# One of four weight sums per quad formed by a plain load and an accumulating transfer instead of a VectorE add

## The chip, the cores and the metric

The kernel runs on one core of one Trainium2 chip. The metric is the device time of one execution in microseconds (us), the median over several runs. The engines are called by the profile's names: PE (TensorE matmul), PEld (TensorE weight load), DVE (VectorE), ACT (ScalarE), POOL (GpSimd), SP (SyncE; SPq is its queue of instructions that issue transfers).

## The reference, cut to what matters

Two layers of a hybrid encoder on 592 tokens (528 of a new stream, 64 of a running one), model width 1024. Each layer is a feed-forward block, a token mixer and a second feed-forward block, all float32. Only the feed-forward blocks meet the change:

```
def _swiglu(x, w_gate, w_up, w_down):
    return (jax.nn.silu(x @ w_gate) * (x @ w_up)) @ w_down
...
h = h + 0.5 * _swiglu(_rmsnorm(h, ln_ffa_w[l]), ffa_w_gate[l], ffa_w_up[l], ffa_w_down[l])
```

`w_gate` and `w_up` are 1024 x 2816, `w_down` is 2816 x 1024.

## The kernel before

**Seven products in place of eight.** Most of a feed-forward block is cast as 2 x 2 blocks of products and computed with seven block products instead of eight (a Strassen-Winograd scheme). One such group is a *quad* (class `Quad`, line 439). For the up side a quad makes one 128-wide column of gate and of up for both halves of the tokens; for the down side it makes two columns of the output. The four blocks of weights of a quad are g1, g2 (`wg`) and u1, u2 (`wu`), each 128 partitions by `nk` slices of 128 floats; `nk` is 4 on the up side, 3 or 2 on the down side. The seven products need seven weights: the raw g1, g2, u2 and four sums, s1 = u1+u2, s2 = s1+g1, s4 = s2+g2, s3 = g1+u1. They are used in the order of `QUAD`: g1, s1, s2, s4, s3, g2, u2, so s3 is the fifth. There are 20 up quads in each of four feed-forward blocks, and 16, 16, 16 and 12 down quads: 140 in all, 80 with nk = 4, 48 with nk = 3, 12 with nk = 2.

**From HBM to PE.** `fetch_quad` (line 568) loads g1, u1, u2, g2 from SP's queue into `braw` (six buffers; the trace calls them wr, the loads are at line 574). `combine` (line 584) forms the four sums on DVE (line 588) into `bzq` (four buffers; the trace calls the sums ws). `convert` (line 593) splits each of the seven weights into a rounded part on ACT (wh, line 603, six buffers) and a remainder on DVE (wl, line 607, six buffers). `product_quad` (line 666) multiplies: for each slice three matmuls of 296 columns (288 in the last block), hi x hi, hi x lo, lo x hi (lines 680 to 682), so 21 x nk matmuls for a quad. A product is accumulated in PSUM onto an earlier one; the next product into the same accumulator is held by a gate until an engine has read the intermediate value (DVE at lines 909 and 1018, ACT at 888 to 898). Those readers stand in DVE's queue among the sums and the remainders.

**Order.** Every engine works its instructions in the order in which they were written. That order comes from a planner (class `Plan`): each piece of work is a generator that yields an engine, an assumed duration, the events that it waits for and the buffers that it needs, and the planner always takes the task that could start first, by its assumed times (a DMA of a slice 190 ns, landing 2000 ns later, a DVE pass 67 ns + n/0.96). On the chip an instruction waits by semaphores for what it needs, and all behind it on its engine wait with it. `bzq` is also used in the token mixers, which hold no quads. POOL's queue holds little in the feed-forward blocks: a power function at each norm, and scaling in the last one.

Of the kernel before, what the change touches and what calls it, by code (L numbers as in the profile page):

```python
# [13 lines left out]
ALU = mybir.AluOpType  # L14
PSUM = bass.MemoryType.PSUM

P = 128
# [18 lines left out]


BLK = ((0, 128), (128, 128), (256, 128), (384, 128), (512, 80))
NT = 52
UK = 4  # L40
LEVELS = (64, 32, 16, 8, 4, 2, 1)

# [73 lines left out]
def ns_dve(n):  # L116
    return 67 + n / 0.96
# [80 lines left out]
def body(ctx: ExitStack, tc: tile.TileContext, a: dict, o: dict):  # L198
    nc = tc.nc
    V, S, G, PE, SP = nc.vector, nc.scalar, nc.gpsimd, nc.tensor, nc.sync  # L200
# [5 lines left out]
    plan = Plan({PE: (200.0, 60.0), V: (220.0, 0.0), S: (265.0, 0.0), G: (100.0, 0.0)}, {G: V})  # L206
    bT = Buf(sb, "T", NT, [P, T], F32, 6)
    bhw = Buf(sb, "hw", 6, [P, HT], F32)
    bzq = Buf(sb, "zq", 4, [P, T], F32)
    braw = Buf(sb, "raw", 6, [P, UK, P], F32)  # L210
# [192 lines left out]
    def near(order):  # L403
        return 1e-3 * order
# [50 lines left out]
    class Mix:  # L455
# [18 lines left out]
        def combine(self, j, x1, x2, y, evs, done):  # L474


            n = self.n
            lo, hi = slice(0, n), slice(n, 2 * n)
            t = yield V, 3 * ns_dve(n), (evs[0], evs[1], evs[3])
            V.tensor_tensor(y[:, lo], x2[:, hi], x1[:, hi], op=ALU.subtract)  # L480
            V.tensor_tensor(x1[:, hi], x1[:, lo], x1[:, hi], op=ALU.subtract)
            V.scalar_tensor_tensor(y[:, hi], x1[:, hi], -1.0, x2[:, hi], op0=ALU.mult, op1=ALU.subtract)
            ends = []
            for p, src, w in ((0, x1, t), (1, y, t), (2, x2, evs[2])):
                ends.append(Ev())
                plan.add(near(self.order + 2 * p), self.split(p, j, src[:, :2 * n], t, w, ends[-1]))
            t = yield V, ns_dve(n), (ends[0], evs[2])
            V.scalar_tensor_tensor(x1[:, lo], y[:, hi], -1.0, x2[:, lo], op0=ALU.mult, op1=ALU.subtract)
            yield "none", 0, (t, ends[1])
            done[2](max(t, ends[1].t))  # L490
            e4 = Ev()
            plan.add(near(self.order + 6), self.split(3, j, x1[:, lo], t, t, e4))
            yield "none", 0, (t, ends[2])
            done[1](max(t, ends[2].t))
            yield "none", 0, (e4,)
            done[0](e4.t)
# [14 lines left out]
    def fetch():  # L511
# [9 lines left out]
        for i, job in enumerate(jobs):  # L521
            if isinstance(job, Quad):
                yield from fetch_quad(i, job, chain)
                continue
            src = job.src.rearrange("(k p) c -> p k c", p=P)
            for k0, k1, u in job.units:
                if job.whole:
                    if i == 0:
                        yield from whole(i, job, src, k0, k1, u, chain)
                    else:  # L530
                        plan.add(near(job.order), whole(i, job, src, k0, k1, u, chain))
                    if i == 0:
                        for b, g in ((0, 1), (1, 1), (2, 1)) if k0 == 0 else ():
                            yield from fetch_x(b, g)
                    continue
                t = yield "DMA", 190 * (k1 - k0), (), (braw,)
                raw = braw.tile(f"wr{i}", [P, k1 - k0, src.shape[2]])
                SP.dma_start(raw, src[:, k0:k1])
                t += 2000.0
                if job.few:  # L540
                    plan.add(near(job.order), convert_few(i, job, u, raw, t, chain))
                else:
                    plan.add(near(job.order), convert(u, raw, chain, braw.put, t))
            if i == 1:
                for b, g in ((3, 0), (4, 0), (3, 1), (4, 1)):
                    yield from fetch_x(b, g)
                t = yield "DMA", 380, ()
                SP.dma_start(cf[:, P:], a["c_f"][:, P:3 * P])
                cf_ev.set(t + 2000)
                load_params()  # L550
# [17 lines left out]
    def fetch_quad(i, job, chain):  # L568
        nk = job.mix.nk
        got = {}  # L570
        for name, src in (("g1", job.wg[0]), ("u1", job.wu[0]), ("u2", job.wu[1]), ("g2", job.wg[1])):
            t = yield "DMA", 190 * nk, (), (braw,)
            raw = braw.tile(f"wr{i}", [P, nk, P])
            SP.dma_start(raw, src)
            got[name] = [raw, Ev(), Ev({"g1": 3}.get(name, 2), braw.put)]
            got[name][1].set(t + 2000.0)
        for name, n in (("s1", 2), ("s2", 2), ("s4", 1), ("s3", 1)):
            got[name] = [None, Ev(), Ev(n, bzq.put)]
        plan.add(near(job.order), combine(i, nk, got))
        for k, ((name, _, _), u) in enumerate(zip(QUAD, job.units)):  # L580
            raw, ev, use = got[name]
            plan.add(near(job.order + k), convert(u, got[name], chain, use.set, ev))

    def combine(i, nk, got):
        for name, p, q in (("s1", "u1", "u2"), ("s2", "s1", "g1"), ("s4", "s2", "g2"), ("s3", "g1", "u1")):
            t = yield V, ns_dve(nk * P), (got[p][1], got[q][1]), (bzq,)
            dst = got[name][0] = bzq.tile(f"ws{i}", [P, nk, P])
            V.tensor_tensor(dst, got[p][0], got[q][0], op=ALU.add)  # L588
            got[name][1].set(t)
            got[p][2].set(t)  # L590
            got[q][2].set(t)

    def convert(u, raw, chain, done, *waits):

        prev, chain[0] = chain[0], Ev()
        split = chain[0]
        n = u.n * P
        t = yield S, ns_act(n), (*waits, prev) if prev else waits, (bhi,)
        if isinstance(raw, list):
            raw = raw[0]  # L600
        u.hi = bhi.tile("wh")
        hi = u.hi[:, :u.n]
        S.activation(hi, raw, AF.Copy)  # L603
        split.set(0.0)
        t = yield V, ns_dve(n), (t,), (blo,)
        u.lo = blo.tile("wl")
        V.tensor_tensor(u.lo[:, :u.n], raw, hi.bitcast(F32), op=ALU.subtract)  # L607
        done(t)
        u.ready.set(t)
# [447 lines left out]
    for e in range(2):  # L1057
        t = const.tile([P, 5 * P], F32, name=f"att{e}")
# [944 lines left out]
```

## Time and profile before

| | |
|---|---|
| median of 3 runs | 2339.91 us (2338.31 to 2341.12) |
| profiled execution, its own time | 2347.44 us |
| span in the profile | 2345.7 us |
| mean granted TensorE clock | 0.992 |
| PE busy | 2271.2 us (97%) |
| DVE busy | 2026.8 us (86%) |
| ACT busy | 1213.5 us (52%) |
| POOL busy | 122.5 us (5%) |
| DMA engines' share | 27.9% (185.50 MB on SP's queue) |

The profiled execution lies 7.5 us over the median, and its span 1.7 us below its own time. Busy times are shares of the span; matmuls overlap each other in the records, so a gap of less than about 0.16 us between two matmuls doesn't show as idle time of PE.

### The profile page before, as it was taken

To read this page: it belongs to the slowest core of one execution; us is meant where nothing else is said; L and a number is where in the kernel's file an instruction comes from. 1 tells how busy PE (TensorE), PEld (TensorE's weight loads), DVE (VectorE), ACT (ScalarE), POOL (GpSimd) and SP (SyncE) were. 2 spreads that over 40 slices of the span, in tenths; PEclk is the share of its full clock that TensorE was granted. 3 is DMA by queue.
4 is the path that set the end of the run, shared out by engine and by line. 5 is a ranking of instruction groups with operands and counts; after the bars stand their busy time and mean duration, and the time that the engine had idled before them with its cause. 6 is when DMAs were issued, how large, how long until landed. Compare 5 with 4: busy or idle time off the path is not lost.

```text
span 2345.7 us, 43539 instructions
## 1 busy us (share of the span) xinstructions
PE 2271.2 (97%) x16199; PEld 2186.0 (93%) x16199; DVE 2026.8 (86%) x4224; ACT 1213.5 (52%) x2488; POOL 122.5 (5%) x167
## 2 busy tenths in 40 slices
PE   8989999999899999999999999999998999999998
PEld 6989999999899899999979999999997998999998
DVE  6989989768976899998989999896789678998995
ACT  4555646446443355564545556464563534554653
POOL 0000000021300000000000000000212000000002
PEclk9999999999999999999999999999999999999999
DMA  4232232332112123323223323323311221333232
GB/s 119 83 96 86 86 95 77 95 80 60 28 46 82 54 82 100 91 82 100 75 70 88 100 84 91 90 80 92 81 44 33 64 86 50 89 101 90 86 96 76
DMA packets 370243, 188.28 MB, mean 80 GB/s; under 512 B 16544, under 2 KB 367568, under 8 KB 370032
## 3 DMA queue, kind: packets, MB, share of 16 engines
q1 hardware_dynamic: 370032, 185.50, 27.9%
q8 instruction: 128, 2.10, 0.4%
q14 instruction: 83, 0.68, 0.1%
HBM read 180.94 MB, written 4.51 MB: 79 GB/s over the span
## 4 chain that ended last, share of the span: by engine, by line
PE 55%; DVE 32%; DMA 7%; issue 4%; ACT 1%; SPq 0%; POOL 0%; DVEq 0%; ACTq 0%
DVE wl L607 8%; PE pq L680 6%; PE pq L682 6%; PE pq L681 6%; DVE ws L588 5%; PE pd L680 3%; DVE h L1018 3%; PE pd L681 3%; PE pd L682 3%; DMA wr<-in_ffa_w_up 2%; DMA wr<-in_ffb_w_up 2%; DVE ql_g L505 2%; PE pa L1385 2%; PE px L654 1%; PE px L656 1%
## 5 line engine op out<-in xcount | busy, mean ns | idle before, releaser
L603 ACT ACTIVATE wh<-ws 128x512 fp32r<-128x512 f32 (+2 forms) x560 | 321.4, 575 | 274.2 <-PE pd L681 119.4
L603 ACT ACTIVATE wh<-wr 128x512 fp32r<-128x512 f32 (+2 forms) x572 | 333.0, 587 | 222.9 <-PE pd L681 89.4
L607 DVE TENSOR_TENSOR wl<-wr,wh 128x512 fp32r<-128x512 f32 (+2 forms) x572 | 358.1, 639 | 6.8 <-ACT wh L603 4.9
L607 DVE TENSOR_TENSOR wl<-ws,wh 128x512 fp32r<-128x512 f32 (+2 forms) x560 | 338.5, 615 | 20.2 <-ACT wh L603 19.1
L680 PE MATMUL pd<-qh_g,wh 128*128 128x296 f32 (+1 forms) x1008 | 306.8, 304 | 11.7 <-DVE h L1018 9.5
L681 PE MATMUL pd<-ql_g,wh 128*128 128x296 f32 (+1 forms) x1008 | 301.9, 300 | 4.1 <-DVE ql_g L505 4.1
L682 PE MATMUL pd<-qh_g,wl 128*128 128x296 f32 (+1 forms) x1008 | 301.2, 299 | 0.0
L680 PE MATMUL pq<-qh_a,wh 128*128 128x296 f32 x960 | 287.8, 300 | 0.7 <-ACT gg L898 0.7
L682 PE MATMUL pq<-qh_a,wl 128*128 128x296 f32 x960 | 286.5, 298 | 0.9 <-DVE wl L607 0.9
L681 PE MATMUL pq<-ql_a,wh 128*128 128x296 f32 x960 | 286.9, 299 | 0.2 <-DVE ql_a L505 0.2
L682 PE MATMUL pq<-qh_b,wl 128*128 128x296 f32 (+1 forms) x960 | 285.0, 297 | 1.0 <-DVE wl L607 0.9
L680 PE MATMUL pq<-qh_b,wh 128*128 128x296 f32 (+1 forms) x960 | 285.6, 298 | 0.0
L681 PE MATMUL pq<-ql_b,wh 128*128 128x296 f32 (+1 forms) x960 | 285.6, 297 | 0.0
L588 DVE TENSOR_TENSOR ws<-wr,wr 128x512 f32<-128x512 f32 (+2 forms) x280 | 172.5, 616 | 48.7 <-DMA wr<-in_ffa_w_up 21.9
L680 PEld LDWEIGHTS pd<-qh_g,wh 128*128 128x128 f32 x1008 | 191.0, 189 | 21.7 <-issue 14.5
L1018 DVE SCALAR_TENSOR_TENSOR h<-pd,h 128x296 f32<-128x296 f32 (+1 forms) x420 | 191.4, 457 | 11.6 <-PE pd L682 10.8
L681 PEld LDWEIGHTS pd<-ql_g,wh 128*128 128x128 f32 x1008 | 191.4, 190 | 4.7 <-DVE ql_g L505 4.7
L682 PEld LDWEIGHTS pd<-qh_g,wl 128*128 128x128 f32 x1008 | 191.1, 190 | 0.0
L681 PEld LDWEIGHTS pq<-ql_a,wh 128*128 128x128 f32 x960 | 180.9, 188 | 1.4 <-DVE ql_a L505 1.2
L682 PEld LDWEIGHTS pq<-qh_a,wl 128*128 128x128 f32 x960 | 180.7, 188 | 1.5 <-DVE wl L607 1.5
L682 PEld LDWEIGHTS pq<-qh_b,wl 128*128 128x128 f32 x960 | 180.5, 188 | 1.7 <-DVE wl L607 1.7
L681 PEld LDWEIGHTS pq<-ql_b,wh 128*128 128x128 f32 x960 | 180.7, 188 | 1.1 <-DVE ql_b L505 1.0
(468 smaller groups left out, 5606.7 us busy)
## 6 DMA issues: line engine op xcount, KB each, us to landing
wr<-in_w_in SPq DMA_DIRECT2D x112, 256.0 KB, 3.1
wr<-in_ffa_w_gate SPq DMA_DIRECT2D x88, 256.0 KB, 3.0
wr<-in_ffa_w_up SPq DMA_DIRECT2D x88, 256.0 KB, 3.2
wr<-in_ffb_w_gate SPq DMA_DIRECT2D x88, 256.0 KB, 3.0
wr<-in_ffb_w_up SPq DMA_DIRECT2D x88, 256.0 KB, 3.2
wr<-in_ffa_w_down SPq DMA_DIRECT2D x96, 192.0 KB, 2.8
wr<-in_ffb_w_down SPq DMA_DIRECT2D x96, 192.0 KB, 2.7
wr<-in_w_out SPq DMA_DIRECT2D x32, 256.0 KB, 3.0
```

The lines of the kernel that those rows point to most:

```text
L505: V.tensor_tensor(ql, src, qh.bitcast(F32), op=ALU.subtract)
L588: V.tensor_tensor(dst, got[p][0], got[q][0], op=ALU.add)
L603: S.activation(hi, raw, AF.Copy)
L607: V.tensor_tensor(u.lo[:, :u.n], raw, hi.bitcast(F32), op=ALU.subtract)
L654: PE.matmul(out[:, :n], u.hi[:, i], xh, start=(j == 0), stop=False)
L656: PE.matmul(out[:, :n], u.lo[:, i], xh, start=False, stop=(j == nk - 1))
L680: PE.matmul(out, u.hi[:, j], xh, start=(new and j == 0), stop=False, skip_group_check=True)
L681: PE.matmul(out, u.hi[:, j], xl, start=False, stop=False, skip_group_check=True)
L682: PE.matmul(out, u.lo[:, j], xh, start=False, stop=(j == nk - 1), skip_group_check=True)
L1018: V.scalar_tensor_tensor(dst, sums[b], sign, dst, op0=ALU.mult, op1=ALU.add)
L1385: PE.matmul(pt[:n, c0 // 2:(c0 + n) // 2], ks[:, c0:c0 + n], qs[:, c0 // 2:(c0 + n) // 2], start=True, stop=True)
```

## The change

The sum s3 leaves `combine`. A new task `load_sum` for each quad takes a `bzq` buffer, loads u1 (`wu[0]`) into it by a plain transfer from SP's queue, and then issues from POOL's queue a second transfer of g1 (`wg[0]`) from HBM with `accum_op=ALU.add` onto the same buffer. The tasks are chained: the first transfer of one isn't planned before that of the task ahead of it (`before`, `after`). In the planner the first counts 190 ns a slice on the DMA, the second is ready 2500 ns later, counts 1000 ns on POOL, and s3 counts as there 4500 ns after that. g1 now has two readers instead of three and u1 one instead of two. For the descriptors of POOL's transfers 2048 bytes a partition are reserved instead of 256, and the pool `T` of general buffers (592 floats a partition each) has 51 instead of 52. The planner is run anew, so the order of all engines can come out otherwise.

```diff
-NT = 52
+NT = 51
...
-            got[name] = [raw, Ev(), Ev({"g1": 3}.get(name, 2), braw.put)]
+            got[name] = [raw, Ev(), Ev({"u1": 1}.get(name, 2), braw.put)]
             got[name][1].set(t + 2000.0)
         for name, n in (("s1", 2), ("s2", 2), ("s4", 1), ("s3", 1)):
             got[name] = [None, Ev(), Ev(n, bzq.put)]
+        prev, sums[0] = sums[0], Ev()
+        plan.add(near(job.order), load_sum(i, nk, job.wu[0], job.wg[0], got["s3"], prev, sums[0]))
         plan.add(near(job.order), combine(i, nk, got))
...
+    sums, begun = [Ev(0)], []
+
+    def load_sum(i, nk, first, second, to, before, after):
+
+        t = yield "DMA", 190 * nk, (before,), (bzq,)
+        dst = to[0] = bzq.tile(f"wa{i}", [P, nk, P])
+        SP.dma_start(dst, first)
+        after.set(0.0)
+        t = yield G, 1000, (t + 2500.0,)
+        G.dma_start(dst, second, accum_op=ALU.add)
+        to[1].set(t + 4500.0)
+
     def combine(i, nk, got):
-        for name, p, q in (("s1", "u1", "u2"), ("s2", "s1", "g1"), ("s4", "s2", "g2"), ("s3", "g1", "u1")):
+        for name, p, q in (("s1", "u1", "u2"), ("s2", "s1", "g1"), ("s4", "s2", "g2")):
...
-    nc = _bacc.Bacc("TRN2", target_bir_lowering=False, num_devices=1, dynamic_dma_scratch_size=256)
+    nc = _bacc.Bacc("TRN2", target_bir_lowering=False, num_devices=1, dynamic_dma_scratch_size=2048)
```

## Rows read from the trace of the kernel before

**Rows 1.** Windows view, four quad stretches: length; busy us (count) PE, PEld, DVE, ACT, POOL; clock; DMA
```profile
53.78:435.54 381.76, 365.46 (x2606) 357.56 (x2605) 351.74 (x739) 216.06 (x432) 1.35 (x4) 0.99 0.30 87
817.26:1186.52 369.26, 363.07 (x2607) 356.16 (x2606) 347.49 (x714) 202.56 (x406) 0.00 (x0) 1.00 0.31 91
1224.33:1594.98 370.65, 363.62 (x2606) 357.01 (x2605) 351.00 (x722) 210.94 (x425) 0.00 (x0) 1.00 0.30 88
1971.45:2305.22 333.77, 328.19 (x2438) 323.66 (x2437) 311.73 (x622) 185.06 (x364) 0.00 (x0) 1.00 0.32 92
sum 1455.44, PE 1420.35 PEld 1394.39 DVE 1361.97 ACT 814.62 POOL 1.35; mean PE 355.09 PEld 348.60 DVE 340.49 ACT 203.66 POOL 0.34
```

**Rows 2.** Timeline of PE inside one stretch: start us, duration us
```profile
1290.04 0.30 PE L680 MATMUL pd<-qh_g,wh 128*128 128x296 f32 x1
...
1291.26 0.30 PE L680 MATMUL pd<-qh_g,wh 128*128 128x296 f32 x1
```

**Rows 3.** Waits of PE: us in total, times, longest us
```profile
PE pd L680 <- DVE h L1018: 13.6, 15, 6.4
PE pq L680 <- DVE u L909: 9.6, 17, 2.5
...
PE pd L681 <- DVE ql_g L505: 4.1, 3, 1.7
```

**Rows 4.** Windows view just after the long stall, and the matmul that ended it
```profile
149.00:152.00 3.00, 2.73 (x11) 2.76 (x12) 2.30 (x6) 0.34 (x1) 0.00 (x0) 0.50 0.59 171
...
149.27 0.58 PE L680 MATMUL pd<-qh_g,wh 128*128 128x296 f32 x1 [6.40 <-DVE h L1018]
```

**Rows 5.** Waits of DVE
```profile
DVE ws L588 <- DMA wr<-in_ffa_w_up: 21.9, 16, 6.6
...
DVE ws L588 <- DMA wr<-in_ffb_w_up: 16.7, 19, 3.5
```

**Rows 6.** Waits of SPq and of ACT
```profile
SPq L574 <- DVE wl L607: 734.9, 232, 16.8
...
ACT wh L603 <- PE pd L681: 208.8, 305, 5.1
```

**Rows 7.** Timeline of DVE: a sum and its follower, four and three slices
```profile
268.26 0.69 DVE L588 TENSOR_TENSOR ws<-wr,wr 128x512 f32<-128x512 f32 x1
268.86 0.69 DVE L607 TENSOR_TENSOR wl<-wr,wh 128x512 fp32r<-128x512 f32 x1
...
1151.13 0.55 DVE L588 TENSOR_TENSOR ws<-wr,wr 128x384 f32<-128x384 f32 x1
1151.60 0.77 DVE L505 TENSOR_TENSOR ql_g<-gg,qh_g 128x592 fp32r<-128x592 f32 x1
```

**Rows 8.** DMA issues: SPq instruction count, KB each, median us from issue to landing
```profile
wr<-in_ffa_w_up SPq DMA_DIRECT2D x88, 256.0 KB, 3.2
...
x<-in_x_prompt SPq DMA_DIRECT2D x6, 256.0 KB, 7.0
```

**Rows 9.** DMA queues: packets, MB, share of 16 engines
```profile
q1 hardware_dynamic: 370032, 185.50, 27.9%
```

**Rows 10.** Timeline of DVE and POOL in the first mixer
```profile
568.89 2.44 POOL L1515 TENSOR_TENSOR st_o<-st_o,mhalf 128x4 f32<-128x4 f32 x2 [28.71 <-DVE st_o L1512]
...
569.34 0.77 DVE L1265 TENSOR_TENSOR l<-l,l 128x592 f32<-128x592 f32 x1
...
572.72 0.83 DVE L1276 SCALAR_TENSOR_TENSOR cmk<-cmk,lnc,cum 128x592 f32<-128x592 f32 x1
...
599.47 1.03 POOL L1681 TENSOR_TENSOR ls<-cf,lah 128x512 fp32r<-128x512 f32 x1
...
600.05 6.08 DVE L1276 SCALAR_TENSOR_TENSOR cmk<-cmk,lnc,cum 128x592 f32<-128x592 f32 x1
...
604.47 1.03 POOL L1681 TENSOR_TENSOR ls<-cf,lal 128x512 fp32r<-128x512 f32 x1
```

## The prediction

> **What bounds the kernel now.** The change touches only quads, so I looked first for the time that quads take. The windows view cut at the first and last quad matmul of each feed-forward block gives four stretches of 381.8, 369.3, 370.7 and 333.8 us, 1455.4 us of the 2345.7 us span; the reader is to see that PE is busy 1420.4 us and DVE 1362.0 us of them, both near full, and POOL 1.35 us [rows 1]. The rest, mixers and norms, has no quad.
>
> The second view is PE's timeline in a spot without gaps. Nine matmuls take 1291.26 - 1290.04 = 1.22 us, so 0.1356 us each at 296 columns [rows 2]. A block has 20 x 4 x 21 up and (3+2+3+3) x 4 x 21 down matmuls, 2604, or 353.1 us at that pace; the last block has 2436, which at 288/296 of the pace is an estimated 321.4 us. Sum 1380.7 us: PE alone would need that. The stretches lose 1455.4 - 1380.7 = 74.7 us over it, and no relief of DVE can give back more than this.
>
> The third view is what PE waited for. In the stretches it is nearly always DVE: the accumulation into h (13.6 us), the reader u (9.6 us), the remainders ql_g (4.1 us) [rows 3]. One of these waits is 6.4 us, and the 3 us behind it run at 0.50 of the granted clock, TensorE's 1.2 GHz level, after that idleness [rows 4]. It stands in the first block, where DVE waited 6.6 us for u1 and u2 behind a burst of small parameter loads [rows 5]. That is about 6.4 + 1.5 = 8 us which a saved add doesn't touch. So some 67 us are open to the change; 27.3 - 6.4 = 20.9 us of them show as waits for those three, the rest lies in gaps that overlapping records hide.
>
> The fourth view is what DVE waited for: 38.6 us of the sums' own wait for u1 and u2 [rows 5]. So DVE has little slack, and a good part of it is transfers that come late, in front of a sum, with the readers of PSUM queued behind. SP's loads in turn wait for `braw` buffers that a remainder on DVE frees (734.9 us, all harmless as long as loads are ahead) [rows 6].
>
> **The change, part by part.**
>
> *Removed: 140 adds on DVE.* The add on four slices starts at 268.26 and its follower at 268.86: 0.60 us. On three slices it is 1151.13 to 1151.60: 0.47 us [rows 7]. Two slices are one step less, an estimated 0.34 us. 80 x 0.60 + 48 x 0.47 + 12 x 0.34 = 48.0 + 22.6 + 4.1 = 74.7 us of DVE, 5.5% of its 1362.0 us. This is DVE time, not kernel time.
>
> *Moved: the release of raw buffers.* u1's buffer comes free after s1 instead of after s3, g1's after s2 and its conversion. The next quad's first load can start earlier; but u2, which s1 needs, is only third in the queue and still waits for a third buffer. I count this as nothing in the sum, and as what pays for busier DMA engines.
>
> *Added on SP: 140 plain loads of u1.* SPq idles for most of a stretch in waits for buffers [rows 6], so issuing is free unless a load stands in front of a raw load while waiting for its `bzq` buffer. Behind it then stand g1, u1, u2, g2 of the next quad, and DVE's s1 waits for those.
>
> *Added on the DMA engines.* 370032 packets took 27.9% of 16 engines in 2345.7 us, 28.3 ns each [rows 9]. Each new operand has 488 slices x 128 partitions = 62464 packets, 110 us of all 16 engines. For the accumulating one I bound the price from once to twice that (it must also fetch what it adds to), 110 to 221 us; together 220 to 331 us in 1455 us of stretches. The share there rises from 0.31 to between 0.46 and 0.54 [rows 1]: no bound by itself, but a raw load that takes 3.2 us from issue to landing [rows 8] can find half of one more in its way. I charge 5 us, with a range of nothing to 25 us: 0.18 us on each of 140 quads at most, of which DVE's slack takes most.
>
> *Added on POOL: 140 instructions that issue the second transfer.* The trace of before has none. Lower bound nothing; nearest rows are POOL's own instructions, 1.03 us for a 512-wide product and 2.44/2 = 1.22 us for a power [rows 10]. At 1.2 us they are 168 us on an engine that is idle in the stretches. The power at each norm stands in the same queue; it waits at most for one such transfer's u1 (3.2 us), five times, when no quad is close: nothing taken, 16 us as far end.
>
> *The chain of one s3.* Plain load 3.2 us [rows 8], POOL 0 to 1.2 us, accumulating transfer between 3.2 us (a plain one) and 7.0 us (the same 256 KB while the start of the kernel loads x) [rows 8]: 6.4 to 11.4 us. I take 8.5 us, nearer the quiet row, because the DMA share stays near a half. A quad lasts 84 x 0.1356 = 11.4 us on PE with nk = 4, 8.5 us with 3, 5.7 us with 2. So the sum has to be started about a quad ahead, in one of four `bzq` buffers, and then the other three sums have fewer to run ahead in. What covers a late s3 is that conversions run ahead of PE: ACT waited 208.8 us for PE to free a weight buffer [rows 6], which it only does when it is six weights ahead, and s3 is one in seven.
>
> *One buffer fewer in `T`.* No row shows a wait for one. Nothing taken; up to 5 us as an estimate of one stalled hand-over per mixer and norm.
>
> *How DVE's relief reaches PE.* If every us of DVE counted, it would give 67 us (PE is then the bound); if only what DVE would have done in its idle time moves, nothing. DVE's queue delays PE in the visible 20.9 us and in hidden gaps; 5.5% less work for an engine that is 94% busy should remove more than a third of the queueing. I take 25 us of the 67, the visible waits and a little more. Sum: 25 - 5 = 20 us off 2347.4 us, so 2327 us for an execution like the profiled one; against the median, which is 7.5 us lower, 2339.9 - 20 = 2320 us.
>
> *POOL against DVE.* In the mixer a DVE instruction with SBUF operands that takes 0.83 us lasted 6.08 us while POOL ran six products of 1.03 us back to back: DVE stood still for as long as POOL streamed. Beside POOL's powers on 4 columns, 2.44 us long, a DVE product took its usual 0.77 us [rows 10]. So it is streaming that blocks, not a busy POOL, and a transfer's issue streams no tensor; I take no blocking. [...]
>
> **The rivals.**
>
> 1. *Larger gain.* The late readers were the whole loss: 35 to 60 us, 2280 to 2305 us. For it: DVE is 94% busy in the stretches [rows 1]. Against: 38.6 us of DVE's idleness waits for transfers, which get no quicker [rows 5].
> 2. *No change.* The freed DVE time becomes waiting for u1 and u2, because the extra traffic delays them by about as much as the add cost (0.5 us a quad). 2335 to 2345 us.
> 3. *Slower: s3 comes late.* If the chain lasts 10 us and runs one buffer at a time, down quads stretch: 48 x (10 - 8.5) + 12 x (10 - 5.7) = 72 + 52 = 124 us, less the gain of 20: about 2440 us. At 9 us it is 24 + 40 - 20 = 44 us, 2384 us. It decides against the change from about 8.7 us, if the planner can't keep two buffers on it. Against it: the conversions' lead.
> 4. *Slower: POOL holds DVE while it writes descriptors, or the reverse.* By the mixer's rows an instruction on POOL costs DVE (6.08 - 0.83)/6 = 0.88 us [rows 10]; 140 x 0.88 = 123 us, less the saved 74.7, is 48 us more for DVE. At one for one that is 2388 us. The break-even is 74.7/140 = 0.53 us a transfer.
>
> **How the numbers follow.** My forecast, 10 to 32 us faster: 0.45, range 2308 to 2330 us. Rival 1: 0.15. Rival 2: 0.14. Rival 3: 0.16. Rival 4: 0.10. 0.2% (4.7 us) is about what a measurement of this kernel can tell from no change: faster 0.45 + 0.15 = 0.60, same 0.14, slower 0.26. The range for eight in ten runs from 2288 us, which leaves out the far end of rival 1 (0.05), to 2385 us, which leaves out half of each slower rival (0.13).
>
> **What would show it.** DVE's sums at the line of `combine` fall from 560 to 420 and its busy time by about 75 us. The four stretches shrink to some 1435 us together, and PE's waits for h and u with them. POOL has 140 more instructions, and DVE's products beside them keep their 0.6 to 0.7 us; longer ones mean rival 4. ACT's conversion of s3 should show no wait for a transfer; if it does, and PE waits for that weight, it is rival 3. DVE's wait for u1 and u2 above 60 us would be rival 2. The prediction fails if the accumulating transfer lands more than about 5 us after its issue while only one buffer serves it.

## The result, and the profile after

The changed kernel takes 2321.7 us (median of 4 runs, 2317.44 to 2327.99), the kernel before 2340.51 us beside it (2338.31 to 2342.73): a ratio of 0.9922 with an interval of 0.9894 to 0.995. Five more rounds gave 2319.07 us and 0.9912 (0.99 to 0.9924), 20.6 us off. The profiled execution took 2317.44 us, its span is 2315.7 us. The profile of before came from an execution 7.5 us above its median, so the two spans lie 30.0 us apart, more than the gain; sizes below go by ratios, and the spans serve to find places.

The windows view of after, cut as in [rows 1]:

```profile
52.99:429.20 376.21, 363.13 (x2606) 357.94 (x2605) 340.05 (x705) 219.00 (x434) 46.29 (x39) 0.99 0.56 129
805.35:1169.66 364.31, 359.15 (x2606) 354.75 (x2605) 336.50 (x681) 203.54 (x407) 46.08 (x36) 1.00 0.58 136
1204.20:1571.55 367.35, 360.36 (x2607) 354.69 (x2605) 339.01 (x691) 211.76 (x428) 44.80 (x35) 1.00 0.57 131
1946.13:2274.47 328.34, 325.85 (x2439) 323.20 (x2437) 299.07 (x591) 185.43 (x364) 39.96 (x31) 1.00 0.59 139
sum 1436.21, PE 1408.49 PEld 1390.57 DVE 1314.63 ACT 819.72 POOL 177.14; mean PE 352.12 PEld 347.64 DVE 328.66 ACT 204.93 POOL 44.28
```

The stretches shrink from 1455.4 to 1436.2 us. Over the 1380.7 us that PE alone would need, they lose 55.5 us where they lost 74.7. DVE is busy 47.3 us less in them, and the share of the DMA engines has gone from 0.31 to 0.57.

Outside the stretches the two spans differ by another 30.0 - 19.2 = 10.8 us, though no sum of a quad lies there. A part of it is the clock at the seam behind the first block (before, then after; PE alone):

```profile
440.00:445.00 5.00, 2.99 (x20) 0.90 0.51 127
445.00:450.00 5.00, 5.00 (x22) 0.50 0.28 83
```

```profile
434.00:439.00 5.00, 3.73 (x29) 1.00 0.77 210
439.00:444.00 5.00, 5.00 (x39) 1.00 0.19 51
```

Before, PE is idle for 2.0 of 5 us there, and the 5 us behind it show a granted clock of 0.50; after, it is idle for 1.3 us, and the 5 us behind it show 1.00. In another execution of the changed kernel PE is idle there for the same 1.3 us, and the 5 us behind it show 0.71; DVE goes 7.52 us there from st_m (L714) to its first q (L1087), 6.02 us in the profile of after. So this part differs from one execution to the next.

What the prediction calls the 1.2 GHz level behind the long stall is, as far as the trace of before shows it, the 0.50 of [rows 4] and a pace: ten matmuls of 296 columns take 2.46 us there, 1.20 columns a ns, where the nine of [rows 2] take 1.22 us, 2.18 columns a ns.

```profile
149.90 0.45 PE L682 MATMUL pd<-qh_g,wl 128*128 128x296 f32 x1
...
152.36 0.45 PE L680 MATMUL pd<-qh_g,wh 128*128 128x296 f32 x1
```

What PE waited for (answers to [rows 3]: the same accumulations, the line numbers 14 higher), then what DVE waited for [rows 5], and what ACT waited for where a transfer of s3 was late:

```profile
PE pq L694 <- DVE u L923: 9.0, 8, 3.1
PE pd L694 <- DVE h L1032: 8.3, 11, 1.9
...
PE pd L695 <- DVE ql_g L505: 3.1, 3, 1.1
PE pq L694 <- ACT gg L902: 2.9, 3, 1.7
```

```profile
DVE wl L621 <- ACT wh L617: 57.6, 76, 1.4
...
DVE ws L602 <- DMA wr<-in_ffa_w_up: 11.0, 15, 2.2
...
DVE ws L602 <- DMA wr<-in_ffb_w_up: 6.1, 9, 2.1
```

```profile
ACT wh L617 <- DMA wa<-in_ffb_w_gate: 11.0, 4, 4.1
...
ACT wh L617 <- DMA wa<-in_ffa_w_gate: 9.4, 4, 2.9
```

PE's three waits fall from 27.3 to 20.4 us; the single stall of 6.4 us [rows 4] is gone as one piece. DVE waits 17.1 us for u1 and u2 where it waited 38.6, and 57.6 us for ACT's rounded weights, where the row of before is

```profile
DVE wl L607 <- ACT wh L603: 24.0, 36, 2.0
```

DVE now reaches a remainder more often before ACT has made its operand, which is what an engine with spare time looks like. ACT waited 23.0 us, nine times, for an s3 that wasn't there yet: 20.4 us in the eight waits of the two rows shown, and one of 2.6 us on the down side. PE shows no wait for a converted weight. But ACT also reads intermediate values for PE, and those reads stand in the same queue. Behind the two longest waits for s3 they came late, and PE stood still for them, 2.6 of its 2.9 us in that row:

```profile
973.20 0.63 ACT L617 ACTIVATE wh<-wa 128x512 fp32r<-128x512 f32 x1 [4.00 <-DMA wa<-in_ffb_w_gate]
...
974.25 0.40 ACT L902 ACTIVATE gg<-pq 128x296 f32<-128x296 f32 x1
...
974.70 0.40 PE L694 MATMUL pq<-qh_b,wh 128*128 128x296 f32 x1 [0.89 <-ACT gg L902]
...
1971.86 0.63 ACT L617 ACTIVATE wh<-wa 128x512 fp32r<-128x512 f32 x1 [4.05 <-DMA wa<-in_ffb_w_gate]
...
1974.40 0.39 ACT L902 ACTIVATE gg<-pq 128x288 f32<-128x288 f32 x1
...
1974.84 0.41 PE L694 MATMUL pq<-qh_b,wh 128*128 128x288 f32 x1 [1.74 <-ACT gg L902]
```

The queues and the issues of after (SP's queue is q1, POOL's q0; for issues the count, KB each and median us from issue to landing):

```profile
q1 hardware_dynamic: 434736, 217.49, 33.5%
q0 software_dynamic: 64704, 31.99, 11.3%
...
wr<-in_ffa_w_up SPq DMA_DIRECT2D x88, 256.0 KB, 3.6
...
wa<-in_ffa_w_up SPq DMA_DIRECT2D x40, 256.0 KB, 3.6
wa<-in_ffa_w_gate POOLq DMA_DIRECT2D x40, 256.0 KB, 4.9
```

An accumulating packet takes 0.113 x 16 x 2315.7 / 64704 = 64.7 ns of an engine, a plain one 0.335 x 16 x 2315.7 / 434736 = 28.5 ns, so 2.27 times as much. Their mean sizes are nearly the same, 494 and 500 bytes. The raw load of u1 and u2 takes 3.6 us in the ffa blocks where it took 3.2 [rows 8]; in the ffb blocks it takes 3.3 where it took 3.2.

### The profile page after: what moved, and what is told of

The parts are those of the page before. It is cut to its first block, busy times and chain, and to the rows that moved or that the text cites. A ratio compares the mean times of both kernels' runs of the same rounds, so it can differ in the third digit from the quotient of the medians.

```text
span 2315.7 us, 44107 instructions
## 1 busy us (share of the span) xinstructions
PE 2252.9 (97%) x16199; PEld 2177.1 (94%) x16199; DVE 1973.5 (85%) x4084; ACT 1216.5 (53%) x2489; POOL 301.5 (13%) x307
## 3 DMA queue, kind: packets, MB, share of 16 engines
q1 hardware_dynamic: 434736, 217.49, 33.5%
q0 software_dynamic: 64704, 31.99, 11.3%
## 4 chain that ended last, share of the span: by engine, by line
PE 74%; DVE 18%; DMA 4%; issue 3%; ACT 1%; SPq 0%; POOL 0%; DVEq 0%; ACTq 0%; POOLq 0%
PE pq L694 10%; PE pq L696 10%; PE pq L695 10%; PE pd L694 5%; PE pd L695 5%; PE pd L696 5%; DVE wl L621 4%; PE pa L1399 2%; PE px L668 2%; PE px L669 2%; PE px L670 2%; PE po L668 1%; PE po L669 1%; PE po L670 1%; PE pg L661 1%
## 5 line engine op out<-in xcount | busy, mean ns | idle before, releaser
L617 ACT ACTIVATE wh<-ws 128x512 fp32r<-128x512 f32 (+2 forms) x420 | 241.4, 575 | 182.0 <-PE pd L695 97.0
L621 DVE TENSOR_TENSOR wl<-ws,wh 128x512 fp32r<-128x512 f32 (+2 forms) x420 | 259.2, 621 | 35.2 <-ACT wh L617 29.7
L694 PEld LDWEIGHTS pq<-qh_b,wh 128*128 128x128 f32 x960 | 181.0, 189 | 3.2 <-ACT gg L902 3.1
L694 PEld LDWEIGHTS pq<-qh_a,wh 128*128 128x128 f32 x960 | 180.7, 188 | 3.2 <-ACT u L908 1.9
```

What stands on the lines that cost most here:

```text
L694: PE.matmul(out, u.hi[:, j], xh, start=(new and j == 0), stop=False, skip_group_check=True)
```

## The experiments

Two theories stood against each other. One: the gain is DVE's time, 140 adds less in the queue where PE's readers stand. The other: the gain is the raw buffers that come free earlier, and the order that the planner makes of it. Beside them stood a question of price: what the transfers take back. Each kernel ran in five rounds beside the kernel before. In the table the gain is (1 - ratio) x 2339.9 us; quads are the stretches of the profile together, with the 37 us or so between the two in the middle, and the rest is what remains of the span. The rest varies from 844 to 855 us among these kernels, though no quad lies in it.

| kernel | median us | ratio (95%) | gain us | quads, rest |
|---|---|---|---|---|
| before | 2339.91 | 1 | 0 | 1493.3, 852.4 |
| the change, again | 2319.07 | 0.9912 (0.99 to 0.9924) | 20.6 | 1472.0, 846.4 |
| DVE's time given back | 2334.22 | 0.9973 (0.9961 to 0.9985) | 6.3 | 1482.9, 851.3 |
| no accumulating transfer | 2302.36 | 0.9842 (0.9827 to 0.9857) | 37.0 | 1453.4, 846.2 |
| plain transfer from POOL | 2308.97 | 0.9861 (0.9847 to 0.9875) | 32.5 | 1460.6, 847.3 |
| before, s3 formed second | 2332.99 | 0.9969 (0.9958 to 0.9979) | 7.3 | 1476.9, 855.1 |
| before, buffers and scratch alone | 2338.41 | 0.9995 (0.9982 to 1.0009) | 1.2 | 1489.9, 852.9 |
| s3 by an add on POOL | 2415.7 | 1.0321 (1.0304 to 1.0339) | -75.1 | 1571.8, 845.0 |
| five sum buffers | 2343.57 | 1.0017 (1.0005 to 1.0029) | -4.0 | 1492.0, 851.7 |
| fewer general buffers alone | 2324.14 | 0.9933 (0.9919 to 0.9946) | 15.7 | 1468.1, 847.9 |
| s1 by transfer too | 2436.33 | 1.0417 (1.0396 to 1.0437) | -97.6 | 1580.5, 851.1 |
| transfers on the up side only | 2336.64 | 0.9984 (0.9971 to 0.9996) | 3.7 | 1482.3, 849.1 |
| accumulated in place | 2321.31 | 0.9919 (0.9906 to 0.9933) | 19.0 | 1470.5, 853.3 |

How far an edit moved the planner's order can be read from the traces. In the two kernels that only alter POOL's transfer, all 4084 instructions of DVE stand in the order of the change (by operation, tiles and shape). With DVE's time given back 3482 of them do, with five sum buffers 3442, with fewer general buffers alone 3989. In the kernel before with s3 second 3402 of 4224 stand in the order of before, with the buffers and the scratch alone 4077.

**The change again**, with no edit.

> The changed kernel once more, beside the kernel before on one chip, so that the later ratios have a neighbour. Forecast step: 20 us off, ratio 0.9915. If the 30 us between the two profiled spans were the real size, the ratio would be 0.987; a ratio over 0.996 would mean that most of the first result was scatter.

2319.07 us. It is the mark for those below.

**DVE's time given back.** In `combine` each quad gets an operation of the same size as the add that was removed, s4 = max(s4, s4), which leaves the values as they are. Transfers and releases stay.

```diff
+            if name == "s4":
+                got[p][2].set(t)
+                got[q][2].set(t)
+                t = yield V, ns_dve(nk * P), (t,)
+                V.tensor_tensor(dst, dst, dst, op=ALU.max)
```

> The changed kernel with 140 needless DVE instructions of the removed add's size (s4 = max(s4, s4) in place, 0.60, 0.47 or 0.34 us each, 74.7 us together); transfers, buffers and results stay. Theory A, the gain is DVE's freed time: the gain goes, and the transfers' cost is left, ratio to the kernel before 0.998 to 1.008, the four stretches back at about 1455 us. Theory B, the gain is the new order, the earlier release of u1 and where the parameter loads fall: the time stays within 5 us of the changed kernel, ratio 0.990 to 0.994.

2334.22 us: 14.3 of the 20.6 us are lost, 6.3 stay. PE's wait for h is 11.7 us here (8.3 in the change), for u 8.2 (9.0). DVE's spare time in front of ACT's weights is gone again:

```profile
DVE wl L628 <- ACT wh L624: 29.6, 44, 2.0
```

DVE's time is the larger part of the net gain, but not all of it. The order is new too, so the 14.3 us aren't DVE's time alone.

**No accumulating transfer.** The planner's task stays, so the plan and the order are those of the change, but POOL issues nothing, and s3 is u1 alone.

```diff
-        G.dma_start(dst, second, accum_op=ALU.add)
```

> The changed kernel without the 140 accumulating transfers on POOL; the plan and the order of every other instruction are the same, s3 is then u1 alone. It measures what these transfers cost. My sum charged 5 us (0 to 25) for all added traffic, so 0 to 5 us faster than the changed kernel, ratio 0.989 to 0.992. If the transfers hold up raw loads or s3, as the slower rival had it, 10 to 25 us faster, ratio 0.981 to 0.987.

2302.36 us: without it the gain would be 37.0 us, so the 140 transfers cost 16.4. The traces say where. The costliest row of DVE's waits for a raw load in front of a sum is now

```profile
DVE ws L601 <- DMA wr<-in_ffb_w_down: 1.4, 1, 1.4
```

in place of 11.0 and 6.1 us, and PE waits 4.5 us for h and 4.8 us for u instead of 8.3 and 9.0. The raw load of u1 and u2 takes 3.1 us from issue to landing in the ffa blocks instead of 3.6. So raw loads that land later beside the transfers are one part of the price. The lateness of s3 itself is another: here ACT shows no wait for it, in place of 23.0 us, and PE none for ACT's read of gg, in place of 2.9. The run takes both away at once and doesn't say how much of the 16.4 us is which.

**Plain transfer from POOL.** The same, but the transfer is kept and only no longer accumulates: g1 overwrites u1, so s3 is g1.

```diff
-        G.dma_start(dst, second, accum_op=ALU.add)
+        G.dma_start(dst, second)
```

> The changed kernel with the second transfer on POOL as a plain one (g1 overwrites u1, so s3 is g1): same order, same issue, same bytes from HBM, no adding. Without the transfer the ratio was 0.984, with it 0.991. If adding is what costs (64.7 ns a packet in the profile after, 28.5 ns on SP's queue), most of the 16 us goes: ratio 0.984 to 0.987, and DVE's wait for u1 and u2 under 8 us. If any further transfer of this size costs as much, ratio 0.989 to 0.992.

2308.97 us, 32.5 us off: the transfers as such cost 37.0 - 32.5 = 4.5 us, about the 5 us of the prediction; that they accumulate costs 32.5 - 20.6 = 11.9 more. Each ratio is uncertain by some 3 us, so the two shares are rough: the 4.5 us aren't clear of nothing, the 11.9 are. DVE waits 3.9 + 1.4 us for raw loads on the up side, and ACT 4.4 us for s3. Its queue and its issues:

```profile
q0 software_dynamic: 10048, 31.99, 4.9%
...
wa<-in_ffa_w_gate POOLq DMA_DIRECT2D x40, 256.0 KB, 3.4
```

The same 31.99 MB go in 10048 packets of 3184 bytes each instead of 64704 of 494, in 4.9% of the engines' time instead of 11.3%. Packets and adding changed together, but SP's queue parts them: its plain packets of 500 bytes cost 0.335 x 16 x 2315.7 / 217.49 = 57.1 us of an engine per MB, the plain ones of 3184 bytes 0.049 x 16 x 2307.9 / 31.99 = 56.6 us, the accumulating ones 0.113 x 16 x 2315.7 / 31.99 = 130.9 us. So it is the accumulating that takes the engines' time, not the size of the packets. POOL's instruction takes 0.75 us instead of 1.30; whether that comes from the number of packets or from the adding isn't parted.

**Before, with s3 formed second.** The kernel before, still with four adds; only their order lets go of g1 and u1 sooner.

```diff
-        for name, p, q in (("s1", "u1", "u2"), ("s2", "s1", "g1"), ("s4", "s2", "g2"), ("s3", "g1", "u1")):
+        for name, p, q in (("s1", "u1", "u2"), ("s3", "g1", "u1"), ("s2", "s1", "g1"), ("s4", "s2", "g2")):
```

> The kernel before with s3 formed second instead of last: u1's buffer comes free after the second add, s3 occupies its sum buffer as early as in the changed kernel, and DVE works as much as before. Theory A (DVE's time): no gain, ratio 0.998 to 1.010. Theory B (early release of u1): most of the change's gain, ratio 0.991 to 0.995.

7.3 us faster, with no transfer and no add saved. This isn't the same quantity as the 6.3 us that stayed when DVE's time was given back: those are left after the transfers have been paid. If the parts simply added up, release and order would be 6.3 + 16.4 = 22.7 us there, against 7.3 here. So the runs bound this part, 7 to 23 us, and don't fix it.

**Before, with the buffers and the scratch of the change alone.**

```diff
-NT = 52
+NT = 51
...
-    nc = _bacc.Bacc("TRN2", target_bir_lowering=False, num_devices=1, dynamic_dma_scratch_size=256)
+    nc = _bacc.Bacc("TRN2", target_bir_lowering=False, num_devices=1, dynamic_dma_scratch_size=2048)
```

> The kernel before with the change's room alone: 51 general buffers instead of 52 and 2048 bytes for descriptors. My sum took nothing, up to 5 us slower: ratio 1.000 to 1.002. It also shows what a new plan does by itself: theory B expects shifts of 10 us and more either way, ratio outside 0.996 to 1.004.

0.9995, nothing measurable.

**s3 by an add on POOL.** The kernel before, with the fourth sum on POOL: DVE is as free as in the change, and no byte more is moved.

```diff
-            t = yield V, ns_dve(nk * P), (got[p][1], got[q][1]), (bzq,)
+            e, ns = (G, ns_pool(nk * P)) if name == "s3" else (V, ns_dve(nk * P))
+            t = yield e, ns, (got[p][1], got[q][1]), (bzq,)
...
-            V.tensor_tensor(dst, got[p][0], got[q][0], op=ALU.add)
+            e.tensor_tensor(dst, got[p][0], got[q][0], op=ALU.add)
```

> The kernel before with s3 added by POOL (a tensor instruction of about 1.0 to 1.3 us for 512 columns) instead of DVE; no transfer is added. DVE is as free as in the changed kernel by count. If a streaming POOL instruction stops DVE for its length, as six of them did in the mixer (0.88 us each), DVE loses 140 x 0.88 = 123 us for 74.7 saved, and the time rises by 20 to 50 us, ratio 1.008 to 1.021. If POOL and DVE share well, the gain of the changed kernel and the spared traffic come, ratio 0.987 to 0.992.

75.1 us slower than before. The timeline of DVE and POOL (start, duration), first of this kernel, then of after:

```profile
900.68 0.55 DVE L608 TENSOR_TENSOR wl<-ws,wh 128x384 fp32r<-128x384 f32 x1
...
901.31 1.02 POOL L589 TENSOR_TENSOR ws<-wr,wr 128x384 f32<-128x384 f32 x1 [8.23 <-DVE wl L608]
...
901.52 1.22 DVE L608 TENSOR_TENSOR wl<-wr,wh 128x384 fp32r<-128x384 f32 x1
```

```profile
1293.05 0.55 DVE L621 TENSOR_TENSOR wl<-wa,wh 128x384 fp32r<-128x384 f32 x1
...
1293.16 1.30 POOL L595 DMA_DIRECT2D wa<-in_ffa_w_gate  x1 [8.08 <-DVE ws L602]
...
1293.89 0.55 DVE L621 TENSOR_TENSOR wl<-wr,wh 128x384 fp32r<-128x384 f32 x1
```

Beside POOL's add a remainder takes 1.22 us instead of 0.55; beside a transfer that POOL issues it takes 0.55 as ever. Over the whole traces, the 26 remainders of three slices that met an add have a median of 1.21 us, the 62 that met a transfer's issue 0.55. PE's wait for h goes to 42.3 us. That is what rival 4 would have looked like.

**Five sum buffers**, and **fewer general buffers alone**. The fifth buffer of `bzq` needs room, so NT goes to 50; the second kernel has NT = 50 and four sum buffers.

```diff
-NT = 51
+NT = 50
...
-    bzq = Buf(sb, "zq", 4, [P, T], F32)
+    bzq = Buf(sb, "zq", 5, [P, T], F32)
```

> The changed kernel with five sum buffers instead of four (and 50 general ones instead of 51). If the long life of s3's buffer robs the other sums of their lead, as the forecast feared, it gains 5 to 15 us over the changed kernel, ratio 0.986 to 0.990. If not, nothing, ratio 0.990 to 0.995.

> The changed kernel with 50 general buffers instead of 51 and nothing else, to part the two edits of the run with five sum buffers (ratio 1.002). If the general buffers were its loss: 0.999 to 1.003. If the fifth sum buffer was (transfers started earlier, in front of the raw loads): 0.990 to 0.993.

Five buffers lose the whole gain, 2343.57 us; NT = 50 alone keeps most of it, 2324.14 us, its interval just meeting that of the change. So the fifth buffer costs some 19 us. DVE's sums wait for raw loads again, as in [rows 5]:

```profile
DVE ws L602 <- DMA wr<-in_ffa_w_up: 28.3, 16, 9.1
...
DVE ws L602 <- DMA wr<-in_ffb_w_up: 15.8, 15, 2.4
```

Whether transfers that start earlier get ahead of the raw loads, or another part of the new plan does it, wasn't told apart.

**s1 by transfer too.** s1 = u1 + u2 gets a second chain of its own, u1 is no longer loaded raw, with five sum buffers and NT = 50.

```diff
+        for to, second in (("s1", job.wu[1]), ("s3", job.wg[0])):
+            prev, sums[0] = sums[0], Ev()
+            plan.add(near(job.order), load_sum(i, nk, job.wu[0], second, got[to], prev, sums[0]))
...
-        for name, p, q in (("s1", "u1", "u2"), ("s2", "s1", "g1"), ("s4", "s2", "g2")):
+        for name, p, q in (("s2", "s1", "g1"), ("s4", "s2", "g2")):
```

> Two sums by transfers: s1 as well (u1 loaded, u2 accumulated onto it); the raw u1 is no longer loaded, five sum buffers. DVE loses a second 74.7 us, POOL has 280 transfers. Theory A, if DVE still held PE: another 10 to 20 us, ratio 0.982 to 0.988. If DVE no longer holds PE, the rest of the 55 us over PE's pace stays and the second step gives under 5 us, ratio 0.989 to 0.993. If s1, used second and needed for s2, comes late, slower than the changed kernel, ratio 0.995 to 1.03.

97.6 us slower than before, 94 more than five buffers alone. What DVE and ACT waited for:

```profile
DVE ws L603 <- DMA wa<-in_ffa_w_up: 62.1, 27, 4.8
...
DVE ws L603 <- DMA wa<-in_ffb_w_up: 51.3, 22, 4.8
```

```profile
ACT wh L618 <- DMA wa<-in_ffb_w_gate: 55.8, 25, 3.9
```

s1 stands at the head of the sums, and s2 and s4 hang on it; with the chain of two transfers in front, DVE stands still for 113 us at these two rows alone, and PE's wait for u rises to 48.0 us. s3 comes late as well, by the row of ACT. This is rival 3, brought about by a sum that is needed early.

**Transfers on the up side only.** The 60 down quads form s3 on DVE again.

```diff
+        if nk == UK:
+            got["u1"][2].n = 1
+            prev, sums[0] = sums[0], Ev()
+            plan.add(near(job.order), load_sum(i, nk, job.wu[0], job.wg[0], got["s3"], prev, sums[0]))
...
-        for name, p, q in (("s1", "u1", "u2"), ("s2", "s1", "g1"), ("s4", "s2", "g2")):
+        for name, p, q in (("s1", "u1", "u2"), ("s2", "s1", "g1"), ("s4", "s2", "g2"), ("s3", "g1", "u1"))[:3 if nk == UK else 4]:
```

> Transfers for the 80 up quads (nk = 4) alone; the 60 down quads keep the DVE add. DVE is spared 48.0 of 74.7 us, the transfers carry 320 of 488 slices. If gain and cost go with the size, two thirds of the gain, ratio 0.993 to 0.995. If the short down quads pay more in late transfers than they save, as good as the change or better, ratio 0.988 to 0.991.

Only 3.7 us, though 48.0 of the 74.7 us of adds are saved. DVE waits 16.6 + 9.5 + 3.7 + 2.5 = 32.3 us for raw loads here; in the change the same rows come to 11.0 + 6.1 + 2.5 = 19.6. PE also waits 5.3 + 3.6 = 8.9 us for ACT's reads of gg, against 2.9 + 0.3 in the change. So the gain isn't in proportion to the adds saved. Why this plan's raw loads and reads are later stays open.

**Accumulated in place.** g1 is accumulated onto the raw u1 once s1 has read it: no second load of u1 and no sum buffer for s3, but the raw buffer is held until s3 is converted.

```diff
+        got["s3"] = [got["u1"][0], Ev(), Ev(1, braw.put)]
+        got["u1"][2] = Ev()
+        plan.add(near(job.order), load_sum(job.wg[0], got["s3"], got["u1"][2]))
...
-        SP.dma_start(dst, first)
...
-        G.dma_start(dst, second, accum_op=ALU.add)
...
+        G.dma_start(to[0], second, accum_op=ALU.add)
```

> s3 in place: no second load of u1, POOL's transfer adds g1 onto the raw u1 once s1 is formed, and s3 is converted from there. 62464 packets less on SP's queue, no sum buffer held by s3; but u1's raw buffer is held until s3 is converted instead of being freed by s1. If the transfers' traffic is what costs, better than the change: ratio 0.984 to 0.989. If the early release of u1's buffer matters as the run with s3 second suggests (7 us), or the transfer, started only after s1, comes late, worse: ratio 0.994 to 1.01.

2321.31 us, the same as the change within the intervals, with SP's traffic back at 185.50 MB. The trace shows a gain and a loss beside each other: less to move, but ACT waits 26.0 + 20.3 + 10.4 + 8.9 = 65.6 us for transfers into the raw buffers. Late s3 and late raw g1 or g2 stand in the same rows here; in the change the two together come to 23.0 + 7.6 = 30.6 us. No version that computes the same beats the change by more than its interval.

## Why the prediction was right, point by point

**The forecast held**: 2320 us, faster, against 2321.7, and the four stretches came out at 1436.2 us where some 1435 were forecast. The sum was 25 us of relief less 5 us of traffic; the runs give other terms with the same difference. The term for traffic was mis-sized: the transfers cost 16.4 us (the change with and without them), three times the 5 us charged, inside the 0 to 25 us of the range. Against that, relief and release together are 37.0 us when nothing is accumulated, and 37.0 - 16.4 is the change's 20.6 us. How the 37.0 us split stays open. If release and order are the 7.3 us of the run with s3 second, about 30 are left for DVE's relief; if DVE's relief is the 14.3 us of the run that gave its time back, about 23 are left for release and order. Both are differences between kernels with different orders. The 25 us taken for the relief lie between. That the errors cancel, 11 us too little for the traffic against 7 us or more for a release that was counted at nothing, is luck.

**Removed adds.** 420 sums instead of 560, as said. DVE's busy time fell by 2026.8 - 1973.5 = 53.3 us, not by about 75. When 140 operations of the same size were given back it was 2029.0 us, 55.5 more, so that is what they show as in this view. The reason is argued only: a record that follows closely begins before the last has ended, 0.69 us of record for 0.60 us of pace [rows 7], so where an add goes and a gap comes, the record behind the gap counts in full.

**Early release**, counted at nothing: this step failed in size. The kernel before gained 7.3 us from the order of its sums alone, and the run that gave DVE's time back leaves up to about 23. Both edits also make the planner anew, so "release" here means release and the order that comes with it.

**The accumulating packet**, bounded between once and twice a plain one: outside the bound, 2.27 times, and by the plain transfer from POOL it is the adding that costs the engines' time, 64.7 ns a packet against 28.5. That such a packet must also fetch what it adds to was the author's reasoning for the bound; no row shows that fetch. The DMA share of 0.56 to 0.59 in the stretches lies above the 0.46 to 0.54 expected for the same reason; the plain packet took 28.5 ns, 28.3 before [rows 9].

**The chain of one s3**: 3.6 us from issue to landing for the plain load and 4.9 for the accumulating one, POOL's instruction included (3.3 to 8.3 over all 140), are 8.5 us, as taken. The sum leaves out the step between them: for the 11 up-side sums of which the trace gives both landings, POOL began 0.7 us after the first landing, and the whole chain took 9.2 us in the median (8.0 to 12.6). That lies beyond the 8.7 us from which rival 3 was to decide, on its condition of one buffer at a time. The condition didn't hold: in 137 of 139 cases the next first transfer was issued before the last s3 was converted. That ACT's conversion would show no wait was wrong: nine came late, 23.0 us. That the conversions' lead covers them was right for the weights, for PE waits for none, but not for ACT's reads behind them in its queue, which cost PE 2.6 us. Rival 3 stays a danger: with a sum needed early it cost 94 us more.

**POOL.** 140 more instructions (167 to 307), 1.30 us each on the up side where 1.2 was taken; issue and plain transfer together cost about 4.5 us. DVE's products beside them keep 0.55 us at three slices. So rival 4 didn't come; an add on POOL, which does stream tensors, shows it at work with 75.1 us, and 1.22 us for a remainder beside the add. POOL's 140 issues take 1.19 to 1.47 us. The choice of no blocking rests on the mixer's rows [rows 10]; why an issue leaves DVE alone and an add doesn't was not shown.

**Buffers and scratch**, counted at nothing: 0.9995 (0.9982 to 1.0009), right.

**Rival 1** (35 to 60 us) would have come true in size without the accumulation: 37.0 us. **Rival 2** named the right counter-force, traffic that delays the raw loads, but the transfers took 16.4 of 37.0 us in all, late s3 included. DVE's wait for u1 and u2 fell to 17.1 us; it was to rise above 60 for that rival.

## What to carry to other kernels

When an engine is the bound by its queue rather than by its sum, count what each saved instruction frees besides its own time (here buffers and a new order, worth 7 to 23 us), and charge the DMA traffic that replaces it by the loads that it delays, not by the DMA engines' idle share. Before moving arithmetic into a transfer, take the transfer away and keep the plan: that one run gives the price, for every other instruction keeps its place. Look also at what stands behind a late operand in its engine's queue: here ACT's reads for PE. And where a planner writes the order, run the neighbouring buffer counts too: one more sum buffer took back 19 us, as much as the change had gained.

## What was not expected of the hardware

- An accumulating packet from POOL's queue, 494 bytes in the mean, took 64.7 ns of a DMA engine, a plain one of 500 bytes from SP's queue in the same kernel 28.5 ns. The same transfer without accumulation went in packets of 3184 bytes, landed in 3.4 us instead of 4.9, and cost the kernel about 4.5 us instead of 16.4. Per MB an engine spent 130.9 us accumulating, and 57.1 or 56.6 us plain, in packets of 500 or 3184 bytes.
- An accumulating transfer that was issued on POOL for 1.30 us left DVE's products at 0.55 us; an add of 1.02 us on POOL made the one beside it 1.22 us.
